# A hybrid decoder layer on one core: two token tiles first in the load queue, compressed-branch sums for four offsets at a time with a gate tile under them, and other places for the last rows of w_o

## The chip, the cores and the metric

The kernel runs on one core of one Trainium2 chip. The metric is the device time of one execution in microseconds (us); lower is better. TensorE multiplies matrices into PSUM, VectorE (DVE), ScalarE (ACT) and GpSimd (POOL) work elementwise, and SyncE (SP) issues most of the loads and stores; each engine takes its instructions in one fixed order.

## The reference

One decoder layer over 1024 tokens of width 1024, all in float32. What matters here:

```python
u = rmsnorm(h, norm_mix_pre[i])
(qa, ka, va, za, ba, aa, qb, kcm, vcm, ksl, vsl, kwi, vwi, gnsa, gmix) = \
    jnp.split(u @ w_in[i], offs, axis=-1)
ya = gdn_mixer(qa, ka, va, za, ba, aa, ...)      # chunked gated delta rule
yb = nsa_mixer(qb, kcm, vcm, ksl, vsl, kwi, vwi, gnsa, ...)   # sparse attention
g_a, g_b = jnp.split(jax.nn.sigmoid(gmix), 2, axis=-1)
mixed = (g_a * (ya @ w_a2d[i]) + g_b * (yb @ w_b2d[i])) @ w_o[i]
h = h + rmsnorm(mixed, norm_mix_post[i])
...                                               # gated MLP, per-layer embedding
def compress_blocks(x, pos, w1, w2):              # for k_cmp and for v_cmp
    ...                                           # blocks of 32 tokens, every 16 tokens: 63 of them
    blocks = blocks + pos[:, None, :]
    flat = jnp.moveaxis(blocks, 3, 2).reshape(B, nc, G, CMP_LEN * d)   # 2048 wide
    return jax.nn.gelu(flat @ w1) @ w2
```

## The kernel before

Every float32 product is split in three. A weight or activation is loaded as float32 ("raw"), ScalarE rounds it to a high part ("hi", whi, w_oh), and VectorE or GpSimd subtracts to get a low part ("lo", wlo, w_ol; all of these are line 313). `mm3` (lines 345 to 347) then issues hi·hi, hi·lo and lo·hi. `stream` does this for one strip of a weight matrix, in the tags "raw", "hi" and "lo" of the pool `wp`, two places each; `weights` does it for the weights `ws` of 288 columns, `resident` for whole rows of a matrix that stay.

The order of the instructions on each engine is laid out when the program is built, by a scheduler that goes by program order, by a simulated timeline and by when a tile's place is free. `tc.issue_after(at)` puts the TensorE instructions of a block behind the instruction `at`; this is how work of one stage is laid under another. A generator such as `project` yields after each half of a product, so a caller can take one step at a time.

*Start.* For each of eight tiles of 128 tokens: x is loaded (two places), normed (`norm_to_T`), turned on TensorE (pT_u) into uh and ul, and multiplied by `ws` (psm, 24 matmuls). All x and `ws` loads stand on SP's queue, as do the strips of w_in (raw) for the projections (pj) that follow. The strips `ws` are loaded in tile 0, after x of token tile 0: four tiles of two row blocks, three pieces each.

*Compressed branch* (`compress`, lines 1106 to 1150). For k and then v, 16 steps m of 128 rows of w1 each: X = one strided slice of cmr plus one column of the position weights (line 1119, VectorE, tile cx), then two matmuls with X (line 1121, tile ph). w1 comes two steps at a time. The generator yields after every four steps, eight times in all; at each yield two steps of the filler generator `first()` follow: q tiles 0 and 1 and one k tile, 12 steps. Then come the gelu (hT), the small product pc, and attention.

*Attention.* 64 items (two groups, eight query tiles, two head pairs, two branches), each with a front (scores ps, softmax Pt) and a back (transposes pt, products po). Under them runs `under()`: two q tiles, the remaining gate tiles of the generator `filler`, the product with w_a2d, and six turns of yb. The share that is due after each item is reckoned by `n_work` (286 units, five for each step) against the cost of the items.

*Merge and output projection.* The products with w_b2d (pab) come in four pairs, each pair with one `stream` of 512 KB; gates gt are loaded from DRAM through four and six buffers, and the merged rows go to mxh and mxl. `open_wo` makes rows 0 to 3 of w_o (k blocks of 128 rows) before that loop, and `ffn` makes rows 4 to 7 after it, in a pool woB, through the two places of "raw". Then `product(t, half)` multiplies token tiles 0 to 2 with rows 0 to 3 (half 0), then with rows 4 to 7 (half 1), 24 matmuls each, into pwo.

Of the kernel before, what the change touches and what calls it, by code (L numbers as in the profile page):

```python
# [7 lines left out]
F32 = mybir.dt.float32  # L8
F32R = mybir.dt.float32r
AF = mybir.ActivationFunctionType  # L10
ALU = mybir.AluOpType
# [4 lines left out]
P = 128  # L16
SEQ = 1024
NT = SEQ // P
DM = 1024
KD = DM // P  # L20
# [12 lines left out]
NWO = 4  # L33


def rows_to_all(ap, n, offset=0):
    return bass.AP(tensor=ap.tensor, offset=ap.offset + offset, ap=[[0, P], [1, n]])
# [257 lines left out]
class Body:  # L295
# [138 lines left out]
    def mixers(self, es_out):  # L434
        nc, tc, io = self.nc, self.tc, self.io
        win = self.dram2d("w_in", DM, DIN)
# [16 lines left out]
        uh = up.tile([P, KD, SEQ], F32R, name="uh")  # L453
        ul = up.tile([P, KD, SEQ], F32R, name="ul")
# [5 lines left out]
        with ExitStack() as e2:  # L460
            sp = self.pool(e2, "ws")
            xw = self.pool(e2, "xw")
            wbc = sp.tile([P, DM], F32, name="wbc")
            for t in range(NT):
                x = xw.tile([P, DM], F32, name="xt", tag="xt", bufs=2)
                nc.sync.dma_start(x, io["x"][0, t * P:(t + 1) * P, :])
                if t == 0:
                    nc.scalar.dma_start(wbc, rows_to_all(io["norm_mix_pre"], DM))
                self.norm_to_T(x, wbc, uh, ul, t, xw, self.psg, f"u{t}")
                if t == 0:  # L470
                    ws = [self.weights(sp, win, k * P, 2, 0, 288, f"ws{k}", 1, pieces=[
                        (0, OFF_VSL, 128), (128, OFF_VWI, 152), (280, OFF_BA, 8)], lo_eng=nc.vector)
                        for k in range(0, KD, 2)]
                    self.load_rows_T([(io["conv_qkv"], 48), (io["cmp_pos_k"], 16), (io["cmp_pos_v"], 16),
                                      (io["gdn_norm"], 1)], self.psg, sp, self.cvw)

                ps = self.psg.tile([P, 512], F32, name="psm", tag="g")
                s = slice(t * P, t * P + P)
                for k in range(KD):
                    self.mm3(ps[:, 0:288], uh[:, k, s], ul[:, k, s], *[w[:, k % 2] for w in ws[k // 2]], k == 0, k == KD - 1)  # L480
                nc.vector.tensor_copy(self.vv[:, t], ps[:, 0:256])
                nc.vector.tensor_copy(self.sg[:, t], ps[:, 256:288])

        def run_all(gen):
            for _ in gen:
                pass
# [49 lines left out]
        def project(off, evac):  # L536

            wh, wl = self.stream(win, 0, KD, off, P)
            for th in range(2):
                s = slice(th * 512, th * 512 + 512)  # L540
                ps = psF[0].tile([P, 512], F32, name="pj", tag="f")
                for k in range(KD):
                    self.mm3(ps, wh[:, k], wl[:, k], uh[:, k, s], ul[:, k, s], k == 0, k == KD - 1)
                    if k == 3:
                        yield
                evac(ps, s)
                yield
# [9 lines left out]
        def gates():  # L557
            for n in range(4, 20):
                yield from gate_tile(n)

        filler = gates()
# [3 lines left out]
        NG = 8  # L565
        self.gdn_prep(0)
        nfill = 0
        for c in range(NC):
            at = self.gdn_scan(c, gates_d, ya_d)
            if c + 1 < NC:  # L570
                at = at, self.gdn_prep(c + 1)
            else:
                at = at, at
# [32 lines left out]
        def q_tile(i):  # L606
            def evac(ps, s):
                for hf in range(2):
                    r = slice(hf * 64, hf * 64 + 64)
                    nc.scalar.activation(self.qb[r, i, s], ps[r], AF.Copy, scale=float(2.0 ** (2 * i + hf + 1) / 8.0))  # L610
            return project(OFF_QB + i * P, evac)
# [3 lines left out]
        def k_tile(n):  # L615
            return project((OFF_KSL, OFF_KWI)[n], lambda ps, s: nc.scalar.activation(self.kk[n][:, s], ps, AF.Copy))

        def first():
            for i in range(2):
                yield from q_tile(i)  # L620
            yield from k_tile(1)

        run_all(k_tile(0))
        fq = first()
        for at in self.compress():
            with tc.issue_after(at):
# [68 lines left out]
            wbs.extend(self.stream(wbd, 0, 4, f * P, 2 * P) for f in (0, 2))  # L695

        todo = under()
        n_work = 5 * (8 + 4 * (16 - NG) + 16) + 6
        cost = lambda i, br: (i + 2 if br == 1 else min(i + 1, 5)) + 1
        total = 4 * sum(cost(i, br) for i in range(NT) for br in (1, 2))  # L700
        items = [(g, i, pr, br) for g in range(2) for i in range(NT) for pr in range(2) for br in (1, 2)]
# [2 lines left out]
        for it in items:  # L704
            g, i, pr, br = it
# [4 lines left out]
            at = self.nsa_front(*it)  # L710
# [39 lines left out]
        for f0 in range(0, KD, 2):  # L750
            wb = wbs.pop(0)
            for th, f in ((0, f0), (0, f0 + 1), (1, f0), (1, f0 + 1)):
                s = slice(th * 512, th * 512 + 512)
# [150 lines left out]
    def gdn_inverse32(self):  # L904
# [6 lines left out]
        self.blk = blk = gp.tile([P, 4, H, P], F32, name="blk")  # L911
        Ls, X = [blk[:, 2 * i:2 * i + 2].rearrange("p a h k -> p (a h k)").rearrange("p (i j) -> p i j", j=32)
                 for i in range(2)]
        tmp = gp.tile([P, 256], F32, name="tmp", tag="T1")
        for hf in range(2):
# [20 lines left out]
            pp = slice(hf * m_, hf * m_ + m_)  # L936
            X_ = X[pp]
            nc.vector.memset(X_, 0.0)
# [166 lines left out]
    def compress(self):  # L1105

        nc, io = self.nc, self.io
        npl = self.pool(self.ces, "cmp")
        for n, s in enumerate("kv"):
            w1 = io[f"cmp_w1_{s}"]  # L1110
            ph = [self.pss.tile([P, 2, NCMP], F32, name="ph", tag="s") for _ in range(2)]
            for m0 in range(0, 16, 2):
                wt = npl.tile([P, 2, 256], F32, name="w1t", tag="w1t", bufs=2)
                nc.sync.dma_start(wt, bass.AP(tensor=w1.tensor, offset=w1.offset + m0 * P * 256,
                                              ap=[[256, P], [P * 256, 2], [1, 256]]))
                for m in (m0, m0 + 1):
                    X = npl.tile([P, 2, 63], F32, name="cx", tag="cx", bufs=2)
                    o = 48 + n * 16 + m
                    nc.vector.tensor_scalar(X, self.cmr[n][:, :, m:m + 497:8], self.cvw[:, o:o + 1], None, ALU.add)
                    for ht in range(2):  # L1120
                        at = nc.tensor.matmul(ph[ht][:, :, 0:63], wt[:, m - m0, ht * P:ht * P + P], X, start=m == 0,
                                              stop=m == 15).ins
                if m0 % 4 == 2:
                    yield at
            hT = npl.tile([P, 2, 2, NCMP], F32, name="hT", tag="hT", bufs=1)
            nc.vector.memset(hT, 0.0)
            for ht in range(2):
                nc.scalar.activation(hT[:, ht, :, 0:63], ph[ht][:, :, 0:63], AF.Gelu_apprx_tanh)
            w2 = npl.tile([P, 2, 2, 64], F32, name="w2t", tag="w2t", bufs=1)
            a = io[f"cmp_w2_{s}"]  # L1130
            for d in range(2):
                nc.sync.dma_start(w2[:, :, d], bass.AP(tensor=a.tensor, offset=a.offset,
                                                       ap=[[64, P], [P * 64, 2], [1, 64]]))
            pc = self.pst.tile([P, 2, NCMP], F32, name="pc", tag="t")
            if s == "k":
                for ht in range(2):
                    nc.tensor.matmul(pc, w2[:, ht], hT[:, ht], start=ht == 0, stop=ht == 1)
                nc.scalar.activation(self.khc, pc, AF.Copy)
                nc.vector.tensor_sub(self.klc, pc, self.khc.bitcast(F32))
            else:  # L1140
                h2 = npl.tile([P, 4, 2, NCMP], F32, name="h2", tag="h2", bufs=1)
                nc.vector.tensor_copy(h2, hT.rearrange("p a b n -> p (a b) n").unsqueeze(2).to_broadcast(
                    [P, 4, 2, NCMP]))
                for g in range(2):
                    for ht in range(2):
                        nc.tensor.matmul(pc[:, g], h2[:, ht * 2 + g].rearrange("p a n -> p (a n)"), w2[:, ht, 0],
                                         start=ht == 0, stop=ht == 1)
                nc.scalar.activation(self.vsc[:, :, 0:64], pc, AF.Copy)
                nc.vector.tensor_sub(self.vsc[:, :, 64:128], pc, self.vsc[:, :, 0:64].bitcast(F32))
        self.ces.close()  # L1150
# [195 lines left out]
    def ffn(self, es_out):  # L1346
        nc, io = self.nc, self.io
# [6 lines left out]
        wq = self.wq = self.pool(hes, "wq", side="right")  # L1354
        cv = wq.tile([P, 4, 2 * NF], F32, name="cv")
        wp = self.pool(self.wes, "woB")
        self.wo += self.resident(wp, "w_o", range(NWO, KD))
        wpost = wp.tile([P, DM], F32, name="wpost")
        nc.scalar.dma_start(wpost, rows_to_all(io["norm_mix_post"], DM))
        wpre = wp.tile([P, DM], F32, name="wpre")  # L1360
# [36 lines left out]
        for t in range(NT):  # L1397
            s = slice(t * P, t * P + P)
            x = wp.tile([P, DM], F32, name="x2", tag="x2", bufs=2)
# [250 lines left out]
```

## Time and profile before

| | |
|---|---|
| three runs, median | 1972.2 us (1970.51 to 1972.72) |
| the profiled execution: its time, its span | 1981.25 us, 1979.5 us |
| instructions | 25890 |
| mean granted clock of TensorE | 0.97 |

The span runs from the first to the last instruction of the profiled execution. Durations are read from it. PE is TensorE's matmul row, PEld its weight loads, which overlap it. A timeline row gives the start, the duration, the engine, the source line, the operation, what it writes and reads, its shape and its count; brackets give the idle time of the engine before it and what ended that. A matmul of 512 columns lasts about 0.39 us, but the next one starts 0.23 us after it.

### The profile page before, as it was taken

What the parts mean: (1) busy time and instruction counts of PE and PEld (TensorE: products, weight loads), DVE (VectorE), ACT (ScalarE), POOL (GpSimd) and SP (SyncE); (2) the same over time, 40 slices, a digit from 0 to 9 for tenths busy, and PEclk for the clock granted to TensorE, in tenths of its full rate; (3) what the DMA queues carried; (4) which work ended last, traced back from release to release, by engine and by line L of the source; (5) the groups of instructions that cost most, each with busy time, mean ns of one, the idle gap of its engine ahead of it and who ended that gap; (6) DMA issues with size and microseconds to landing.
All of it is one profiled execution on the core that took longest, in us unless ns stands there. A gap on an engine that the chain in (4) does not pass through costs nothing. (4 is left out here: it accounts for less than half of the span.)

```text
span 1979.5 us, 25890 instructions
## 1 busy us (share of the span) xinstructions
PE 1856.0 (94%) x9247; PEld 1537.6 (78%) x9247; DVE 1235.3 (62%) x2365; ACT 921.9 (47%) x1818; POOL 702.0 (35%) x537
## 2 busy tenths in 40 slices
PE   7999989999989999999999969999999999999998
PEld 6788778888878878778777857787877877777786
DVE  4437943341367667686684488776867774868643
ACT  4344223333267667676663234444444444346432
POOL 2132212223122212231153045666766665545200
PEclk9998989999989999999999979999999999999999
DMA  5124333323310110110063212323332348236201
GB/s 163 33 72 123 81 98 85 92 76 88 98 33 17 43 38 28 42 61 22 22 223 133 82 64 65 117 91 101 104 104 91 101 142 284 80 111 227 98 35 43
DMA packets 182847, 178.68 MB, mean 90 GB/s; under 512 B 27773, under 2 KB 133566, under 8 KB 182718
## 3 DMA queue, kind: packets, MB, share of 16 engines
q1 hardware_dynamic: 180496, 170.33, 27.5%
q10 hardware_dynamic: 2222, 6.69, 0.9%
q8 instruction: 73, 1.20, 0.2%
q14 instruction: 56, 0.46, 0.1%
HBM read 132.65 MB, written 44.34 MB: 89 GB/s over the span
## 5 line engine op out<-in xcount | busy, mean ns | idle before, releaser
L345 PE MATMUL pj<-uh,whi 128*128 128x512 f32 x640 | 263.5, 412 | 7.5 <-DVE y L515 5.8
L347 PE MATMUL pj<-uh,wlo 128*128 128x512 f32 x640 | 258.9, 404 | 0.0
L346 PE MATMUL pj<-ul,whi 128*128 128x512 f32 x640 | 258.6, 404 | 0.0
L313 POOL TENSOR_TENSOR wlo<-raw,whi 128x1024 fp32r<-128x1024 f32 x48 | 116.9, 2437 | 324.6 <-ACT whi L324 263.8
L345 PEld LDWEIGHTS pj<-uh,whi 128*128 128x128 f32 x640 | 123.7, 193 | 34.6 <-issue 4.4
L313 POOL TENSOR_TENSOR whl<-s,whl 128x512 fp32r<-128x512 f32 x88 | 126.4, 1444 | 59.0 <-ACT whl L1331 59.0
L347 PEld LDWEIGHTS pj<-uh,wlo 128*128 128x128 f32 x640 | 123.3, 193 | 29.0
L346 PEld LDWEIGHTS pj<-ul,whi 128*128 128x128 f32 x640 | 123.8, 193 | 26.1
L313 POOL TENSOR_TENSOR wdhl<-wd,wdhl 128x512 fp32r<-128x512 f32 x66 | 99.0, 1510 | 80.4 <-ACT wdhl L1331 78.9
L313 POOL TENSOR_TENSOR whl<-raw,whl 128x512 fp32r<-128x512 f32 x66 | 105.3, 1597 | 50.9 <-ACT whl L1331 50.3
L313 DVE TENSOR_TENSOR whl<-araw,whl 128x512 fp32r<-128x512 f32 x77 | 86.7, 1133 | 55.3 <-ACT whl L1331 55.2
L345 PE MATMUL q<-mxh,whl 128*128 128x512 f32 x264 | 104.8, 400 | 3.4 <-ACT u L106 2.2
L1243 DVE TENSOR_TENSOR Tl<-pt,Th 128x512 fp32r<-128x512 f32 (+1 forms) x152 | 92.6, 617 | 23.6 <-ACT Th L1242 19.8
L1213 ACT ACTIVATE Pt<-Pt,nm 128x640 f32<-128x640 f32 (+7 forms) x128 | 93.0, 728 | 30.2 <-DVE nm L1211 29.7
L346 PE MATMUL q<-mxl,whl 128*128 128x512 f32 x264 | 104.9, 397 | 0.0
L347 PE MATMUL q<-mxh,whl 128*128 128x512 f32 x264 | 104.1, 397 | 0.2 <-POOL whl L313 0.2
L1242 ACT ACTIVATE Th<-pt 128x512 fp32r<-128x512 f32 (+1 forms) x152 | 79.2, 538 | 51.7 <-PE po L1246 35.6
L324 ACT ACTIVATE whi<-raw 128x1024 fp32r<-128x1024 f32 x48 | 50.5, 1053 | 80.3 <-PE pj L346 54.4
L1239 PE MATMUL pt<-ident,Pt 128*128 128x128 f32 x528 | 82.9, 277 | 2.9 <-DVE Tl L1243 1.3
L126 DVE SCALAR_TENSOR_TENSOR yg<-c,cv,yg 128x1 f32<-128x1 f32 (+2 forms) x88 | 81.3, 928 | 0.9 <-ACT yg L123 0.9
L1331 ACT ACTIVATE whl<-s 128x512 fp32r<-128x512 f32 x88 | 54.7, 624 | 56.9 <-PE n L347 44.1
L1205 PE MATMUL ps<-kst,qs 128*128 128x512 f32 (+3 forms) x192 | 70.4, 369 | 6.7 <-DVE mx L1208 4.9
(533 smaller groups left out, 5138.7 us busy)
## 6 DMA issues: line engine op xcount, KB each, us to landing
raw<-in_w_up SPq DMA_DIRECT2D x44, 512.0 KB
raw<-in_w_in SPq DMA_DIRECT2D x40, 512.0 KB
araw<-acts SPq DMA_DIRECT2D x35, 512.0 KB
acts<-sd SPq DMA_DIRECT2D x44, 256.0 KB
gates_d<-yz SPq DMA_DIRECT2D x40, 256.0 KB
acts<-yv SPq DMA_DIRECT2D x33, 256.0 KB
gt<-gates_d SPq DMA_DIRECT2D x32, 256.0 KB
wd<-in_w_down SPq DMA_DIRECT2D x7, 1024.0 KB
```

Source lines behind the costliest of these rows:

```text
L126: self.body.nc.vector.scalar_tensor_tensor(y, src, w, y, ALU.mult, ALU.add)
L313: return eng.tensor_sub(lo, src, hi.bitcast(F32)).ins
L324: nc.scalar.activation(hi, raw, AF.Copy)
L345: nc.tensor.matmul(ps, lh, rh, start=start, stop=False, skip_group_check=more)
L346: nc.tensor.matmul(ps, lh, rl, start=False, stop=False, skip_group_check=more)
L347: nc.tensor.matmul(ps, ll, rh, start=False, stop=stop, skip_group_check=more)
L1205: nc.tensor.matmul(ps[:, 0:n], qs[:, hh], kh, start=True, stop=False)
L1213: nc.scalar.activation(Pt[:, hh, 0:nk], Pt[:, hh, 0:nk], AF.Exp, scale=2.0 ** -(h0 + hh + 1), bias=nm[:, br, hh:hh + 1], accum_out=rs[:, b ...
L1239: nc.tensor.transpose(pt[:, b, hh], Pt[:, hh, (b0 + b) * P:(b0 + b + 1) * P], self.ident)
L1242: nc.scalar.activation(Th[:, 0:m], pt[:, 0:m], AF.Copy)
L1243: nc.vector.tensor_sub(Tl[:, 0:m], pt[:, 0:m], Th[:, 0:m].bitcast(F32))
L1331: self.nc.scalar.activation(hi, src, AF.Copy)
```

## The change

Four edits. x of token tiles 0 and 1 is put on SP's queue ahead of the strips `ws`, and those come as two tiles of four row blocks (three pieces each) in place of four tiles of two. In `compress`, w1 comes four steps at a time, X is made for four steps by two additions of two tensors (one for each of the two groups g), and the clearing of hT is cut to its one padded column. After q and k tiles, `first()` goes on with four steps of `filler`, that is with one gate tile, and `n_work` counts one gate tile less (266 units). Rows 6 and 7 of w_o are loaded into a place of the tags "hi" and "lo" of `wp`, where the merge's w_b2d parts lie, and rows 4 and 5 into "raw" as before.

```diff
--- before.py
+++ after.py
@@ -461,23 +461,32 @@
             sp = self.pool(e2, "ws")
             xw = self.pool(e2, "xw")
             wbc = sp.tile([P, DM], F32, name="wbc")
+            xs = {}
+
+            def load_x(t):
+                xs[t] = xw.tile([P, DM], F32, name="xt", tag="xt", bufs=2)
+                nc.sync.dma_start(xs[t], io["x"][0, t * P:(t + 1) * P, :])
+
+            load_x(0)
+            load_x(1)
             for t in range(NT):
-                x = xw.tile([P, DM], F32, name="xt", tag="xt", bufs=2)
-                nc.sync.dma_start(x, io["x"][0, t * P:(t + 1) * P, :])
+                if t > 1:
+                    load_x(t)
+                x = xs.pop(t)
                 if t == 0:
                     nc.scalar.dma_start(wbc, rows_to_all(io["norm_mix_pre"], DM))
                 self.norm_to_T(x, wbc, uh, ul, t, xw, self.psg, f"u{t}")
                 if t == 0:
-                    ws = [self.weights(sp, win, k * P, 2, 0, 288, f"ws{k}", 1, pieces=[
+                    ws = [self.weights(sp, win, k * P, 4, 0, 288, f"ws{k}", 1, pieces=[
                         (0, OFF_VSL, 128), (128, OFF_VWI, 152), (280, OFF_BA, 8)], lo_eng=nc.vector)
-                        for k in range(0, KD, 2)]
+                        for k in range(0, KD, 4)]
                     self.load_rows_T([(io["conv_qkv"], 48), (io["cmp_pos_k"], 16), (io["cmp_pos_v"], 16),
                                       (io["gdn_norm"], 1)], self.psg, sp, self.cvw)
 
                 ps = self.psg.tile([P, 512], F32, name="psm", tag="g")
                 s = slice(t * P, t * P + P)
                 for k in range(KD):
-                    self.mm3(ps[:, 0:288], uh[:, k, s], ul[:, k, s], *[w[:, k % 2] for w in ws[k // 2]], k == 0, k == KD - 1)
+                    self.mm3(ps[:, 0:288], uh[:, k, s], ul[:, k, s], *[w[:, k % 4] for w in ws[k // 4]], k == 0, k == KD - 1)
                 nc.vector.tensor_copy(self.vv[:, t], ps[:, 0:256])
                 nc.vector.tensor_copy(self.sg[:, t], ps[:, 256:288])
 
@@ -619,6 +628,8 @@
             for i in range(2):
                 yield from q_tile(i)
             yield from k_tile(1)
+            for _ in range(4):
+                yield next(filler)
 
         run_all(k_tile(0))
         fq = first()
@@ -695,7 +706,7 @@
             wbs.extend(self.stream(wbd, 0, 4, f * P, 2 * P) for f in (0, 2))
 
         todo = under()
-        n_work = 5 * (8 + 4 * (16 - NG) + 16) + 6
+        n_work = 5 * (8 + 4 * (15 - NG) + 16) + 6
         cost = lambda i, br: (i + 2 if br == 1 else min(i + 1, 5)) + 1
         total = 4 * sum(cost(i, br) for i in range(NT) for br in (1, 2))
         items = [(g, i, pr, br) for g in range(2) for i in range(NT) for pr in range(2) for br in (1, 2)]
@@ -1109,21 +1120,23 @@
         for n, s in enumerate("kv"):
             w1 = io[f"cmp_w1_{s}"]
             ph = [self.pss.tile([P, 2, NCMP], F32, name="ph", tag="s") for _ in range(2)]
-            for m0 in range(0, 16, 2):
-                wt = npl.tile([P, 2, 256], F32, name="w1t", tag="w1t", bufs=2)
+            for m0 in range(0, 16, 4):
+                wt = npl.tile([P, 4, 256], F32, name="w1t", tag="w1t", bufs=2)
                 nc.sync.dma_start(wt, bass.AP(tensor=w1.tensor, offset=w1.offset + m0 * P * 256,
-                                              ap=[[256, P], [P * 256, 2], [1, 256]]))
-                for m in (m0, m0 + 1):
-                    X = npl.tile([P, 2, 63], F32, name="cx", tag="cx", bufs=2)
-                    o = 48 + n * 16 + m
-                    nc.vector.tensor_scalar(X, self.cmr[n][:, :, m:m + 497:8], self.cvw[:, o:o + 1], None, ALU.add)
+                                              ap=[[256, P], [P * 256, 4], [1, 256]]))
+
+                X = npl.tile([P, 4, 2, 63], F32, name="cx", tag="cx", bufs=2)
+                v = self.cmr[n].rearrange("p g (n m) -> p m g n", m=8)[:, m0 % 8:m0 % 8 + 4, :, m0 // 8:m0 // 8 + 63]
+                o = 48 + n * 16 + m0
+                for g in range(2):
+                    nc.vector.tensor_tensor(X[:, :, g], v[:, :, g], self.bc(self.cvw[:, o:o + 4], 63), ALU.add)
+                for m in range(m0, m0 + 4):
                     for ht in range(2):
-                        at = nc.tensor.matmul(ph[ht][:, :, 0:63], wt[:, m - m0, ht * P:ht * P + P], X, start=m == 0,
-                                              stop=m == 15).ins
-                if m0 % 4 == 2:
-                    yield at
+                        at = nc.tensor.matmul(ph[ht][:, :, 0:63], wt[:, m - m0, ht * P:ht * P + P], X[:, m - m0],
+                                              start=m == 0, stop=m == 15).ins
+                yield at
             hT = npl.tile([P, 2, 2, NCMP], F32, name="hT", tag="hT", bufs=1)
-            nc.vector.memset(hT, 0.0)
+            nc.vector.memset(hT[:, :, :, 63:64], 0.0)
             for ht in range(2):
                 nc.scalar.activation(hT[:, ht, :, 0:63], ph[ht][:, :, 0:63], AF.Gelu_apprx_tanh)
             w2 = npl.tile([P, 2, 2, 64], F32, name="w2t", tag="w2t", bufs=1)
@@ -1354,7 +1367,8 @@
         wq = self.wq = self.pool(hes, "wq", side="right")
         cv = wq.tile([P, 4, 2 * NF], F32, name="cv")
         wp = self.pool(self.wes, "woB")
-        self.wo += self.resident(wp, "w_o", range(NWO, KD))
+        for ks, tag in (((4, 5), "raw"), ((6,), "hi"), ((7,), "lo")):
+            self.wo += self.resident(wp, "w_o", ks, place=(self.wp, tag))
         wpost = wp.tile([P, DM], F32, name="wpost")
         nc.scalar.dma_start(wpost, rows_to_all(io["norm_mix_post"], DM))
         wpre = wp.tile([P, DM], F32, name="wpre")
```

## Rows read from the trace of the kernel before

**Rows 1.** The page, part 1: busy time, share of the span, instructions.
```profile
PE 1856.0 (94%) x9247; PEld 1537.6 (78%) x9247; DVE 1235.3 (62%) x2365; ACT 921.9 (47%) x1818; POOL 702.0 (35%) x537
```

**Rows 2.** Timeline of SyncE's queue, start: start us, us, what.
```profile
1.25 9.60 SPq L334 DMA_DIRECT2D raw_ws<-in_w_in  x12
10.89 0.94 SPq L466 DMA_DIRECT2D xt<-in_x  x2
```

**Rows 3.** Timeline of all engines, start; in brackets idle before and releaser.
```profile
13.86 0.68 ACT L338 ACTIVATE hi_ws<-raw_ws 128x576 fp32r<-128x576 f32 x1 [1.18 <-DMA raw_ws<-in_w_in]
...
14.58 0.76 DVE L313 TENSOR_TENSOR lo_ws<-raw_ws,hi_ws 128x576 fp32r<-128x576 f32 x1 [0.98 <-ACT hi_ws L338]
...
19.21 1.06 PE L374 MATMUL pT_u<-ident,xs_u 128*128 128x128 f32 x8 [2.90 <-DVE ra_u L353]
...
26.00 0.29 PE L346 MATMUL psm<-lo_ws,uh 128*128 128x288 f32 x1
...
26.14 0.29 PE L347 MATMUL psm<-hi_ws,ul 128*128 128x288 f32 x1
```

**Rows 4.** DMA view, first 40 us: GB/s in slices of one us.
```profile
GB/s 0 16 254 287 416 328 81 136 157 133 203 209 142 256 373 336 344 328 258 111 135 369 160 291 137 215 245 199 315 273 217 173 352 70 12 0 0 0 123 377
```

**Rows 5.** Timeline of TensorE, compressed branch.
```profile
512.89 2.19 PE L1121 MATMUL ph<-cx,w1t 128*128 128x126 f32 x16
...
520.52 2.19 PE L1121 MATMUL ph<-cx,w1t 128*128 128x126 f32 x16
522.46 0.48 PE L345 MATMUL pj<-uh,whi 128*128 128x512 f32 x1
...
531.96 0.82 PE L1121 MATMUL ph<-cx,w1t 128*128 128x126 f32 x4 [1.63 <-DVE cx L1119]
...
535.94 0.39 PE L347 MATMUL pj<-uh,wlo 128*128 128x512 f32 x1
...
547.30 2.19 PE L1121 MATMUL ph<-cx,w1t 128*128 128x126 f32 x16
551.38 1.13 PE L1121 MATMUL ph<-cx,w1t 128*128 128x126 f32 x8 [1.89 <-DVE cx L1119]
554.09 2.08 PE L1121 MATMUL ph<-cx,w1t 128*128 128x126 f32 x8 [1.58 <-DVE cx L1119]
...
560.29 0.44 PE L1205 MATMUL ps<-kst,qs 128*128 128x128 f32 x1 [1.32 <-issue]
...
567.07 0.22 PE L1205 MATMUL ps<-kst,qs 128*128 128x128 f32 x1
```

**Rows 6.** Line 1119, the sums X: ns min/median/max, first and last start.
```profile
L1119 DVE TENSOR_SCALAR cx<-cm,cvw x32: 320/334/2225, 477.9 to 554.0; 128x126 f32<-128x126 f32 x32
```

**Rows 7.** Timeline of all engines, the first of the late sums.
```profile
529.24 2.91 DVE L1119 TENSOR_SCALAR cx<-cm,cvw 128x126 f32<-128x126 f32 x3
529.29 2.48 POOL L313 TENSOR_TENSOR wlo<-raw,whi 128x1024 fp32r<-128x1024 f32 x1 [12.73 <-ACT whi L324]
```

**Rows 8.** Attention in 22 stretches of 20 us: two of them, and the sum.
```profile
580.00:600.00 20.00, 18.44 (x110) 15.60 (x109) 16.01 (x61) 15.70 (x48) 6.18 (x9) 1.00 0.11 27
...
780.00:800.00 20.00, 17.95 (x112) 15.36 (x110) 17.23 (x74) 16.51 (x55) 8.36 (x9) 0.97 0.11 34
...
sum 440.00, PE 419.52 PEld 355.25 DVE 307.57 ACT 302.25 POOL 98.67; mean PE 19.07 PEld 16.15 DVE 13.98 ACT 13.74 POOL 4.48
```

**Rows 9.** Timeline of TensorE, start of the output projection.
```profile
1046.84 0.39 PE L345 MATMUL pwo<-w_oh,mxh 128*128 128x512 f32 x1
...
1069.49 1.65 PE L345 MATMUL pwo<-w_oh,mxh 128*128 128x512 f32 x3 [3.42 <-ACT w_oh L1310]
...
1075.18 0.40 PE L347 MATMUL pwo<-w_oh,mxl 128*128 128x512 f32 x1
```

**Rows 10.** Timeline of ScalarE, the same stretch.
```profile
1054.88 1.06 ACT L1310 ACTIVATE w_oh<-raw 128x1024 fp32r<-128x1024 f32 x1 [0.84 <-DVE mxl L313]
...
1068.38 1.06 ACT L1310 ACTIVATE w_oh<-raw 128x1024 fp32r<-128x1024 f32 x1 [11.50 <-DMA raw<-in_w_o]
```

## The prediction

> **What bounds the kernel now.** I read the page's busy times first: TensorE is busy for 94% of the span and no other engine for more than 62% [rows 1]. So the time is TensorE's work plus its pauses, 124 us of them (1979.5 less 1856.0), and a change that leaves the matmuls alone can only earn pauses, or stretches in which matmuls are spaced as at the lower of the clock's two levels. The reader should look at three places, because the change has one part in each. At the start [rows 2 to 4] the weights wait for the DMA queue and the second token tile waits behind them. In the compressed branch [rows 5 to 7] the filler runs out two steps of the generator before the branch does, and TensorE then waits for VectorE. At the start of the output projection [rows 9, 10] TensorE waits for the last rows of w_o. Between the last two lies attention, 440 us in which TensorE is busy for 419.5 [rows 8]; it matters because the change takes filler out of it.
>
> **Part 1, the start.** Nothing is computed differently. SP issues 12 loads of ws over 9.6 us and only then the second token's x [rows 2]. The last quarter of ws is rounded at 13.86 and its low part is ready at 15.34 (14.58 plus 0.76) [rows 3]; the first tile's matmuls can then end, and TensorE waits 2.90 us until 19.21 for the second token's norm. That token's last matmul starts at 26.14 [rows 3]. After the change x of token 1 is ahead of ws, so its norm and transposes lie under the wait for ws; in exchange ws comes later by one load of 512 KB and in halves instead of quarters. In the slices of one us that follow the first loads 254 to 416 GB/s moved [rows 4]; 0.52 MB at 350 GB/s is 1.5 us. So the second half lands 1.5 us later, at about 15.4. Rounding it takes ScalarE about 1.2 us, estimated from 0.68 us for a tile of half the size, and VectorE about 1.4, from 0.76: 18.0. Eleven of token 0's 24 matmuls are left then (the second half's twelve, less the first, which needs no low part), 1.5 us at the spacing of 0.13 to 0.14 us that its neighbour at 26.00 has to 26.14. Token 1 follows at once: 24 matmuls, 3.2 us, and token 2's 8 transposes, 1.0 us (as token 1's at 19.21), which had also been done by 26.14. That gives 23.7, a gain of 2.4 us. I take off 1.4 because matmuls that begin after a longer wait will run at the lower clock longer: gain 1.0 us. Bounds: +4 if x1 costs ws nothing and the clock is up in time; -2 if the halves come a further 3 us late. Third and later x loads still wait for a place of two, and the w_in loads stand behind them on SP as before; TensorE has projections to do from then on, so I price that at nothing, and at 1 us if that cover were gone (it is in the bounds).
>
> By the Trainium skill, "DMA: Bandwidth & Descriptors", section "Queues, rings and completion order", a DMA engine takes the descriptors of one queue's ring in order; by that ws waits for all of x1 and the sum for this part stays at 1.0. If the two shared the engines instead, so that ws lost nothing, it would be 2.5 by the same working. No row here separates the two.
>
> **Part 2, the compressed branch.** Eight groups of 16 matmuls run, four for k and four for v, and after each two filler steps. One group with its filler takes 7.63 us (512.89 to 520.52), of which 1.94 the group and 5.69 the two steps [rows 5]. There are 12 steps of filler, so groups 7 and 8 had none. The change adds four, one gate tile, so that all eight are covered.
>
> What is removed. (a) At 531.96 TensorE has waited 1.63 us for X. From there to 535.94 four sums (0.48 us) and eight filler matmuls start; the eight take 3.5 us where 5.69 for 24 would make it 1.9. Together 3.2. The cause is visible on VectorE: X takes 0.33 us at the median but 2.2 at the most [rows 6], and just here three of them take 2.91 us, beside a rounding by GpSimd of 2.48 [rows 7]. X had two buffers of one offset each, so it could be made only one offset ahead. (b) From 547.30 to 567.07 are 19.77 us [rows 5]. The work in them at the full clock: 32 sums at 1.94 per 16, 3.9; 16 matmuls of pc and ps, about as wide as the sums, 1.9; 12 filler matmuls, 2.85. That is 8.65, so 11.1 are lost, in waits of 1.89, 1.58 and 1.32 us and a few under 1 us, and in half-clock matmuls. With the gate tile under groups 7 and 8 and X made four offsets at a time and two groups ahead (7.6 us ahead, against a worst X of 2.5), all of it closes except the wait of 1.32 before the first scores, where pc, the rounding of q and the scores follow each other and no filler is queued. I let that wait cost 1.0 more in clock. So 3.2 + 11.1 - 1.3 - 1.0 = 12.0 us.
>
> What is added. The X sums are 2 instructions on VectorE for 4 offsets instead of 4; at 252 elements each I estimate 0.4 us, from 0.33 us for 126, so VectorE does less, and it is off the path. The w1 loads are 8 of 512 KB in place of 16 of 256 KB, with as many bytes; two groups are ahead, 15 us for a load, so nothing. The smaller memset is off the path too. The gate tile brings one w_in load, one rounding by ScalarE and GpSimd (2.5 us) and two stores on SP, all of which were in attention; on SP they go ahead of the last w1 loads, whose cover is the same 7.6 us.
>
> What is given back. The four steps, 11.4 us, leave attention. Its 64 items share 56 steps of filler now and 52 afterwards, so 12 instead of 8 items go without. Over 440 us TensorE pauses 20.5 us there [rows 8]. Four more items, at 0.3 us (the mean pause for each item) to 1.3 (the wait before the first scores [rows 5]), are 1 to 5 us; I take 3. So attention shrinks by about 8.4 of the 11.4, and part 2 earns 9.0. Bounds: 13.0 with no clock loss and nothing reopened; 0.6 if attention does not shrink at all.
>
> **Part 3, w_o.** Rows 4 to 7 are loaded through two places of "raw". Their rounding can begin at 1054.88, when VectorE has done the last mxl, because only then the tiles for them are free [rows 10]. So raw is held until then, rows 6 and 7 are loaded after it, and row 6 is rounded at 1068.38 after 11.50 us of idle time on ScalarE that a DMA ended [rows 10]. TensorE starts the first half at 1046.84; 84 matmuls (72 of the first half, 12 of rows 4 and 5) last until 1066.07, 0.23 us each. It waits 3.42 us until 1069.49, and 13 matmuls until 1075.18 take 5.69 us instead of 2.97 [rows 9]: 3.42 + 2.72 = 6.1 lost. After the change rows 6 and 7 are loaded into places that the merge's third weight pair gives back; 48 merge matmuls before 1046.84, at 0.23 us, put that at about 1035.6, so the loads are there by 1054.88. Four roundings of 1.06 us end by 1059.1, and the low parts (1.4 us on VectorE, estimated from 0.76 for 576 columns [rows 3], and 2.5 on GpSimd as in [rows 7], two each) by about 1062 to 1064. Row 6 is wanted at 1066.1, row 7 at 1067.5. Gain 6.0; bounds 6.1 and 0 (the loads go out only after 1054.88 all the same). SP's wait for those two places stands ahead of at most the last gate loads; those have four and six buffers.
>
> **Sum.** 1.0 + 9.0 + 6.0 = 16.0 us. The profiled execution took 1981.25 us (span 1979.5), so it would take 1965. The median of the runs shown is 1972.2, 9.05 lower; the same difference gives **1956 us**.
>
> **The rivals.** *A, the forecast*, 1949 to 1962; chance 0.50. *B, attention does not shrink*: VectorE and ScalarE are the real limit there, filler was free, and its 11.4 us come back as pauses. For it: VectorE and ScalarE are each busy around 70% [rows 8]. Against: TensorE is at 95%. 1.0 + 0.6 + 6.0 = 7.6: 1964.6 us; chance 0.17. *C, X stays late*: VectorE makes X only just before use, and GpSimd still holds it up, so that (a) and the wait of 1.89 with its clock remain, about 6 us: 1962 us; chance 0.12. The Trainium skill, "SBUF — State Buffer", section "Who interferes with whom", speaks for it: a VectorE instruction with two SBUF inputs is blocked by a GpSimd instruction that reads SBUF for the whole of it, and the new X has two SBUF inputs. The trace agrees that X was held up as long as GpSimd ran [rows 6, 7]. *D, part 3 does not happen*, because rows 6 and 7 are still issued only after 1054.88: 1.0 + 9.0 = 10.0, 1962 us; chance 0.10. *E, slower*: in attention the clock falls. Two stretches of 20 us show it: 18.44 busy still had a granted clock of 1.00, 17.95 had 0.97 [rows 8]. With less filler more stretches look like the second. One hundredth over 440 us costs 4.4 us, so from a fall of the mean by 0.036 on the 16.0 are gone, and a fall by 0.055 makes 1980. Against: even the second stretch, the emptiest before 980, has 0.97, and 11.4 us less in 440 moves the busy share by 2.6% at most. Chance 0.07. *F*, the instruction order changes elsewhere and eats it, within 4 us of before; 0.04.
>
> **How the numbers follow.** The time is that of A, 1956. A's own range is 1949 to 1962: the upper bounds of the parts (4 + 13.0 + 6.1) would give 1949. B, C and D lie at 1962 to 1965, so 1949 to 1967 leaves out about 0.11 for E and F and some tails of the others. A measurement of this kernel tells about 0.2%, 4 us, from no change. Faster needs less than 1968: A to D, less a part of B's and D's tails, 0.83. Slower by 0.2%: E and a little of F, 0.07. Same: 0.10.
>
> **What will show it.** Right: TensorE's rows have no wait for X, and after group 8 comes a gate tile's pj; attention's pauses rise by less than 5 us from 20.5; no TensorE wait for w_oh, and row 6's load is issued before 1050; the second token's transposes come before the first token's last psm. Wrong: attention is as long as before (B); X rows of 2 us next to TensorE waits (C); an SP load of w_o behind w_up (D); a mean granted clock that falls by over 0.03 in attention (E). What I cannot see is the order that instructions get on each engine; if it moves work in stages that the diff does not touch, the forecast fails there.

## The result and the profile after

The changed kernel takes 1958.95 us at the median of nine runs (1954.95 to 1967.18), the kernel before 1973.14 in nine runs taken in turn with them. The ratio is 0.9921 [0.9906, 0.9935], which is 15.6 us less (14.2 by the two medians). The forecast was 1956 us, 16.2 less. The profiled execution took 1955.27 us, its span 1953.5. The page's busy times, as in [rows 1]: TensorE 20.8 us less.

```profile
PE 1835.2 (94%) x9247; PEld 1522.0 (78%) x9247; DVE 1226.0 (63%) x2347; ACT 919.8 (47%) x1816; POOL 708.2 (36%) x537
```

One execution of one kernel differs from the next by several us (spans of 1962.5 to 1975.9 us among 35 runs of the kernel before), so a stage's length is compared below over several profiles. Windows of the changed kernel by stage: compressed branch (first ph to first ps), attention (to the last po), merge (to the first pwo), output projection (to the last pwo). After the time come the busy times of the engines, then the granted clock, DMA share and GB/s.

```profile
479.10:553.70 74.60, 71.77 (x381) 60.69 (x379) 19.34 (x22) 24.65 (x40) 14.58 (x7) 1.00 0.30 87
553.70:978.00 424.30, 403.01 (x2445) 341.56 (x2446) 298.66 (x1060) 295.86 (x764) 95.37 (x115) 0.99 0.10 32
978.00:1031.30 53.30, 47.49 (x198) 37.40 (x197) 45.70 (x50) 33.42 (x55) 30.61 (x18) 0.97 0.71 237
1031.30:1121.90 90.60, 90.60 (x418) 75.35 (x417) 41.78 (x68) 27.99 (x60) 17.80 (x19) 1.00 0.31 106
```

The same stages of the kernel before, repeated (the experiment with no edit):

```profile
478.10:550.40 72.30, 65.05 (x334) 54.13 (x332) 23.19 (x40) 21.60 (x35) 12.32 (x5) 0.95 0.33 90
550.40:984.20 433.80, 415.48 (x2493) 352.34 (x2494) 304.12 (x1060) 299.27 (x769) 97.92 (x116) 0.98 0.11 33
984.20:1037.30 53.10, 48.94 (x197) 38.53 (x196) 45.63 (x50) 33.32 (x55) 30.70 (x18) 0.94 0.64 218
1037.30:1131.70 94.40, 92.56 (x418) 76.26 (x417) 40.56 (x68) 28.24 (x60) 16.89 (x19) 0.98 0.32 113
```

The branch has become longer, since it holds 11.4 us more filler, and attention shorter; the two together take 498.9 us for 506.1. The reader should watch the clock column beside the idle time: the branch loses 4.4 us of idle time and its clock goes from 0.95 to 1.00.

*Start.* Rows of SyncE, ScalarE and TensorE, which answer to [rows 2, 3]:

```profile
0.80 0.87 SPq L468 DMA_DIRECT2D xt<-in_x  x2
1.72 7.44 SPq L334 DMA_DIRECT2D raw_ws<-in_w_in  x6
...
12.58 1.17 ACT L338 ACTIVATE hi_ws<-raw_ws 128x1152 fp32r<-128x1152 f32 x1
12.67 1.91 PE L374 MATMUL pT_u<-ident,xs_u 128*128 128x128 f32 x8
...
21.37 1.03 PE L374 MATMUL pT_u<-ident,xs_u 128*128 128x128 f32 x8
...
24.64 0.63 PE L374 MATMUL pT_u<-ident,xs_u 128*128 128x128 f32 x4 [1.45 <-DVE xs_u L365]
```

The wait of 2.90 us for the second token tile's norm is gone: that tile is turned at 12.67, under the wait for ws, and the third tile at 21.37. The next long wait is for VectorE's next norm (1.45 us). The second half of ws is rounded at 12.58, before the last quarter of [rows 3] at 13.86; the row has no idle time, so ScalarE did not wait for this load.

*Branch.* TensorE's timeline for [rows 5]; then ScalarE, VectorE and GpSimd ahead of the first scores:

```profile
505.08 1.95 PE L1135 MATMUL ph<-cx,w1t 128*128 128x126 f32 x16
...
512.48 1.94 PE L1135 MATMUL ph<-cx,w1t 128*128 128x126 f32 x16
...
549.89 1.06 ACT L324 ACTIVATE whi<-raw 128x1024 fp32r<-128x1024 f32 x1 [5.14 <-PE pj L346]
...
551.02 2.34 POOL L313 TENSOR_TENSOR wlo<-raw,whi 128x1024 fp32r<-128x1024 f32 x1 [12.40 <-ACT whi L324]
551.33 0.27 ACT L1161 ACTIVATE vsc<-pc 128x128 fp32r<-128x128 f32 x1
551.48 1.72 ACT L1191 ACTIVATE qs<-qb 64x256 fp32r<-64x256 f32 x4
...
552.00 2.52 DVE L313 TENSOR_TENSOR qs<-qb,qs 64x256 fp32r<-64x256 f32 x2
...
553.75 0.30 PE L1218 MATMUL ps<-kst,qs 128*128 128x128 f32 x1 [2.87 <-issue]
...
554.57 0.33 PE L1218 MATMUL ps<-kst,qs 128*128 128x128 f32 x1 [0.41 <-DVE qs L313]
```

A group of 16 matmuls takes 1.95 us and no group waits. But the wait before the first scores, 1.32 us in [rows 5], has grown to 2.87 + 0.41. VectorE's two low parts of qs took 0.87 us in the kernel before and take 2.52 here. The row of before:

```profile
559.77 0.87 DVE L313 TENSOR_TENSOR qs<-qb,qs 64x256 fp32r<-64x256 f32 x2 [0.17 <-ACT qs L1178]
```

The sums X, beside [rows 6]:

```profile
L1132 DVE TENSOR_TENSOR cx<-cm,cvw x16: 626/660/2694, 469.8 to 530.2; 128x252 f32<-128x252 f32 x16
```

They still take up to 2.69 us, and nobody waits.

*Output projection*, SyncE and ScalarE, for [rows 10]:

```profile
1026.05 0.86 SPq L1320 DMA_DIRECT2D raw<-in_w_o  x2
...
1039.13 1.06 ACT L1323 ACTIVATE w_oh<-raw 128x1024 fp32r<-128x1024 f32 x1 [0.84 <-DVE mxl L313]
...
1041.05 1.99 ACT L1323 ACTIVATE w_oh<-raw 128x1024 fp32r<-128x1024 f32 x2
```

SyncE in the kernel before:

```profile
1057.53 5.96 SPq L1307 DMA_DIRECT2D raw<-in_w_o  x2
```

The last two loads go out at 1026.05, 5 us before the stage begins (before at 1057.53, some 11 us behind its begin), the four roundings follow one another, and TensorE has no pause in the stage (90.60 of 90.60 us).

### The profile page after: what moved, and what is told of

Same layout as the page of the kernel before. It is cut to its first block, busy times and chain, and to the rows that moved or that the text cites. A ratio compares the mean times of both kernels' runs of the same rounds, so it can differ in the third digit from the quotient of the medians.

```text
span 1953.5 us, 25809 instructions
## 1 busy us (share of the span) xinstructions
PE 1835.2 (94%) x9247; PEld 1522.0 (78%) x9247; DVE 1226.0 (63%) x2347; ACT 919.8 (47%) x1816; POOL 708.2 (36%) x537
## 5 line engine op out<-in xcount | busy, mean ns | idle before, releaser
L313 POOL TENSOR_TENSOR whl<-s,whl 128x512 fp32r<-128x512 f32 x88 | 131.6, 1505 | 57.2 <-ACT whl L1344 57.2
L1294 POOL TENSOR_TENSOR tm<-tm 128x128 f32<-128x128 f32 x32 | 14.7, 460 | 196.2 <-DVE tm L1292 160.8
```

Source lines behind the costliest of these rows:

```text
L313: return eng.tensor_sub(lo, src, hi.bitcast(F32)).ins
L1294: nc.gpsimd.tensor_add(tm[:, 0], tm[:, 0], tm[:, 1])
```

## The experiments

**Each part alone.** The kernel before once more; the start edit alone; the sums and the gate tile alone; the places of w_o alone.

> The kernel before, unchanged, taken once more. Spread theory (the two profiled executions, 1979.5 and 1953.5, lie 26 us apart while the medians lie 14 us apart, because executions of one kernel differ by some us in stages that nothing touches): a span some 4 to 10 us below 1979.5, ratio 1.000, and the first sums of the compressed branch begin 2 to 6 us ahead of 486.4. Start theory (the start edit is worth 7 us, as the first sums' 486.4 against 479.1 suggest): they begin within 1 us of 486.4 again.

> Only the start edit: two x tiles first in the queue and ws in two halves. Spread theory: 1 to 3 us faster than before (ratio 0.998 to 1.0), and what the first 25 us of the trace gain is what stays. Start theory: about 7 us faster, ratio 0.9965.

> Only the sums for four offsets, the gate tile under them and the filler count. Forecast: 9.0 us faster, ratio 0.9954, attention shorter by 8 to 9 us. Rival B (attention does not shrink): 0.6 us, ratio 0.9997. Rival C (sums stay late): about 3 us, ratio 0.9985.

> Only the places of w_o rows 6 and 7. Forecast: 6.0 us faster, ratio 0.997, and no wait of TensorE for w_oh. Rival D (the loads still go out late): ratio 1.000.

The kernel before took 1971.7 us beside these four. No edit: 0.9999 [0.9986, 1.0013]. Start: 1.0000 [0.9988, 1.0013]. Sums and gate tile: 0.9965 [0.9951, 0.9979], 6.9 us less. w_o: 0.9988 [0.9975, 1.0002], 2.4 us less. The unchanged kernel's profile has a span of 1963.7 for 1979.5 us and its first sums at 478.1 for 486.4: more than was expected of the spread, and not the start edit's doing.

The sum of the parts, 9.3 us, is short of 15.6, by only a little more than the intervals allow. The profile of the start edit shows one reason: its merge took 56.2 us where the kernel before took 53.0 and 53.1. TensorE waits there for a rounding of the next weights, 4.18 us, where it waited 2.36 to 2.44 for a product of the gates before, and its clock in the merge is 0.91 for 0.94. VectorE's products of the gates stand in another order than before. The lines, TensorE in the merge, of the start edit, then of the changed kernel:

```profile
1015.94 0.80 PE L345 MATMUL pab<-ybh,whi 128*128 128x512 f32 x1 [4.18 <-ACT whi L324]
```
```profile
1008.61 0.50 PE L345 MATMUL pab<-ybh,whi 128*128 128x512 f32 x1 [4.00 <-DVE gt L769]
```

So an edit at the start re-orders work 900 us later. The changed kernel has VectorE's order of before, waits 4.00 us at this place as well, and its merge takes 53.3 at a clock of 0.97: the wait alone is not the 3 us. With w_o alone its stage takes 90.7 us at a clock of 1.00, as in the changed kernel.

**The two halves of part 2.** Sums without the gate tile: X and w1 as in the change, `first()` and `n_work` as before. From its diff against the kernel before:

```diff
-            for m0 in range(0, 16, 2):
...
+            for m0 in range(0, 16, 4):
...
+                for g in range(2):
+                    nc.vector.tensor_tensor(X[:, :, g], v[:, :, g], self.bc(self.cvw[:, o:o + 4], 63), ALU.add)
```

> X and w1 for four offsets at a time, without the gate tile. If late X is what costs (part 2, a, and the X waits of 1.89 and 1.58 us in groups 7 and 8), TensorE has no wait of over 0.3 us for cx, and the kernel is 3.2 to 7 us faster, the rest of the 11.1 us staying because nothing lies under groups 7 and 8 and the gelu. If X stays late beside GpSimd (rival C), waits for cx of 1 us and more remain and the time is within 2 us of before.

0.9946 [0.9933, 0.9959], 10.6 us less: more than with the gate tile (the intervals overlap), and more than the 3.2 to 7 that were expected. In the branch it is 7.6 us; the merge, which the edit does not touch, took 51.1 us for 53.0. Windows (branch, attention) and TensorE's timeline:

```profile
485.20:549.90 64.70, 60.84 (x334) 51.77 (x332) 18.16 (x22) 21.44 (x35) 11.95 (x5) 0.99 0.33 92
549.90:982.90 433.00, 414.67 (x2493) 351.78 (x2494) 304.61 (x1060) 299.15 (x769) 97.71 (x116) 0.99 0.10 33
```
```profile
541.20 3.73 PE L1124 MATMUL ph<-cx,w1t 128*128 128x126 f32 x32
...
547.53 1.10 PE L1148 MATMUL pc<-w2t,h 128*128 128x64 f32 x8 [2.61 <-DVE h L1144]
549.89 0.45 PE L1207 MATMUL ps<-kst,qs 128*128 128x128 f32 x1 [1.25 <-issue]
```

Groups 7 and 8, with nothing under them, take 3.73 us together: X is ready. What is left is 2.61 us behind the gelu and 1.25 before the scores. The gate tile with the sums as before (`first()` and `n_work` alone):

> The gate tile under groups 7 and 8 and n_work less by 20, with X and w1 as before. If missing filler is what costs, the branch loses its pauses behind group 6 (about 7.9 us of 11.1 gross) and attention gives 3 us back: about 5 us faster, with the X waits of rows 5 (1.63 us) left. If filler was free in attention (rival B), attention stays at 433.8 us, the branch becomes some 4 us longer, and the time is the same or up to 4 us longer than before.

0.9988 [0.9975, 1.0], 2.4 us less. Windows (branch, attention) and the wait that stays:

```profile
481.20:561.20 80.00, 75.52 (x381) 62.48 (x380) 24.47 (x40) 24.68 (x40) 14.98 (x7) 0.98 0.32 88
561.20:988.30 427.10, 405.35 (x2445) 343.89 (x2446) 298.20 (x1060) 296.12 (x764) 95.33 (x115) 0.98 0.10 32
```
```profile
526.77 0.71 PE L1123 MATMUL ph<-cx,w1t 128*128 128x126 f32 x4 [1.63 <-DVE cx L1121]
```

The two stages together take 507.1 us: nothing won. The expected 5 us did not come.

**The changed kernel again, and the wait before the scores.**

> The changed kernel unchanged, once more. If the three parts add up as they were measured alone (0.0, -7.2 and -1.5 us), the ratio is 0.995 to 0.996. If the first result of 0.9921 stands, the parts together save about 6 us more than alone, and the granted clock of attention will again be about 0.99 against 0.98.

0.9923 [0.9906, 0.9939]: the first result stands. Branch 74.6, attention 427.5 us at a clock of 0.98; so attention of this one kernel differs by 3 us and 0.01 of clock between two executions. The first query tile's qs made earlier (comments added here):

```diff
+            if n == 4:                         # behind group 5
+                self.nsa_q(0, 0)
...
     def nsa_q(self, g, i):
-        nc, npl = self.nc, self.np_            # a pool that is made behind the branch
+        nc, npl = self.nc, self.nsar           # a pool that is open in the branch
```

> The changed kernel with the first query tile's rounding (qs of group 0, tile 0) made under group 5 of the compressed branch, not behind pc. If qs is what the 2.87 us before the first scores wait for, this wait and the 0.41 behind it fall to under 0.5 us, the clock in the 20 us that follow rises from 0.91 to about 1.00, and the kernel is 3 to 5 us faster than the changed one in the same call. Rival: the first scores wait for pc and its copies instead, or the pause moves behind the first softmax, which has no filler either; then it is within 1 us of the changed kernel.

0.9909 [0.9892, 0.9926]; by the medians 2.3 us under the repeat of the changed kernel, measured beside it, where 3 to 5 were expected (the intervals overlap). The branch takes 71.6 us, all of them busy:

```profile
479.00:550.60 71.60, 71.60 (x382) 60.62 (x380) 19.20 (x21) 23.16 (x37) 13.61 (x7) 1.00 0.30 87
```

The 3.28 us are gone from the branch, and no further wait opened in it. So qs was what the scores waited for. The clock in the 20 us behind the first scores did not rise to 1.00 as expected: it is 0.91, as in the first profile of the changed kernel (0.83 in its repeat).

**Without the gate tile, and the filler spread.** The changed kernel less the gate tile; then also, with qs early:

```diff
-                next(fq, None)
-                next(fq, None)
+                for _ in range((1, 1, 1, 2, 1, 2, 2, 2)[n]):
+                    next(fq, None)
+            if n == 5:
+                self.nsa_q(0, 0)
```

> The changed kernel without the gate tile in the branch (first() and n_work as before); start, sums and w_o as changed. If the gate tile earns nothing once X comes early (the branch grows by 9.9 us with it, attention shrinks by 6.3 on average), this is 2 to 5 us faster than the changed kernel: ratio to before 0.990 to 0.991, branch 64.7 us, attention 433. If the forecast's working holds (the tile closes pauses that X alone leaves, and 8.4 of 11.4 us come back), it is 3 to 6 us slower than the changed kernel: ratio 0.9945 to 0.996.

> The changed kernel without the gate tile; the 12 filler steps stand behind the eight groups as 1, 1, 1, 2, 1, 2, 2, 2, so that two of them lie under each of the two chains gelu to pc, and the first qs is made under group 6. If the pauses of 2.61 and 1.25 us that the sums alone left (behind gelu, and before the first scores) are all that is left in the branch, it takes 60 to 61 us with TensorE busy throughout, attention 433, and the kernel is about 4 us faster than without the gate tile alone, 1950 to 1953 us by the time of before in these calls. Rival: with only one step between groups X or w1 comes late (waits for cx or the load of 0.5 us and more), and the branch stays at 64 to 66 us.

Without the tile 1955.96 us, 0.9912 [0.9892, 0.9933], 2 to 3 us under the changed kernel; its branch takes 65.5 us, attention 433.8. That is on the side of no gain from the tile, though the intervals overlap. Its windows (branch, attention):

```profile
479.40:544.90 65.50, 61.68 (x333) 52.55 (x331) 18.14 (x22) 21.40 (x35) 11.96 (x5) 0.97 0.33 91
544.90:978.70 433.80, 415.33 (x2493) 352.32 (x2494) 304.33 (x1060) 299.43 (x769) 97.91 (x116) 0.98 0.10 33
```

Spread: 1952.08 us, **0.9887 [0.9866, 0.9908]**, the fastest kernel here, 21 us under before. Windows and timeline of it:

```profile
478.20:538.60 60.40, 60.40 (x333) 51.61 (x332) 14.14 (x19) 18.97 (x32) 11.23 (x6) 1.00 0.33 90
538.60:972.30 433.70, 414.64 (x2495) 351.32 (x2495) 307.30 (x1062) 301.02 (x772) 98.92 (x115) 0.99 0.11 34
```
```profile
537.80 1.00 PE L1159 MATMUL pc<-w2t,h 128*128 128x64 f32 x8
538.61 0.31 PE L1218 MATMUL ps<-kst,qs 128*128 128x128 f32 x1
...
542.77 0.34 PE L1218 MATMUL ps<-kst,qs 128*128 128x128 f32 x2
```

The same twelve steps as before cover the branch whole: one step between two groups is enough for X, and two lie under each gelu. 60.4 us is what was expected.

**The start.** Only x of two tiles first, ws in quarters; and the spread kernel with quarters.

> Only x of token tiles 0 and 1 first in the queue; ws in quarters as before. In the four profiles with the whole start edit the last psm ends at 62.9 and the first gate scores of the linear attention come at 80.8 to 81.3; without it at 63.4 to 66.0 and at 79.6 to 87.3. If the order of x does this, psm ends at 62.9 or earlier and the second stage begins by 81. If the halves of ws do it (six issues in 7.44 us for twelve in 9.60), psm ends at 64 or later. In time both are within 3 us of before.

> As the kernel with the spread filler, but ws in quarters again: x of two tiles first, twelve pieces of ws behind it. If the 5.0 us that the order of x saved alone belong to the start (against 0.0 with halves), this is 2 to 5 us faster than with halves: ratio to before 0.986 to 0.988, with a second stage that begins before 81. If halves are the better (12.58 against 14.61 for the rounding of the last piece) the second stage begins 2 to 5 us later, at 83 to 86, and the ratio is 0.989 to 0.991. If the 5.0 lay in a later stage (the linear attention took 170.3 against 172.5 to 177), the ratio stays within 0.001 of 0.9887.

0.9975 [0.9959, 0.9991], 5.0 us where at most 3 were expected, and 0.9918 [0.9897, 0.994]. SyncE and ScalarE of the first of the two:

```profile
1.71 10.71 SPq L334 DMA_DIRECT2D raw_ws<-in_w_in  x12
...
14.61 0.68 ACT L338 ACTIVATE hi_ws<-raw_ws 128x576 fp32r<-128x576 f32 x1 [1.13 <-DMA raw_ws<-in_w_in]
```

With quarters behind two x tiles the last quarter is rounded at 14.61 and 14.76, the second stage (first pss) begins at 86.3 and 84.8 us; with halves it begins at 80.8 to 81.3 in six profiles, with the old start at 79.6 to 87.3 (mean 84.0) in six. So the order of x alone gains nothing here, and with the halves it is about 3 us on average; the halves with the old order were not run.

Against that, the linear attention (first pz to last pu) took 170.3 and 170.7 us in these two kernels and 172.5 to 177.2 in all others, which is about where the 5.0 us of the first come from. The traces show how: TensorE's instructions stand there in another order in these two (the same in both), and its waits for T (tile pu) come to 3.5 and 3.7 us, in all others to 6.0 to 8.3. Why this edit leads to that order, no run separates. What was expected of halves at the second stage's begin held. The spread kernel with quarters is 3 us slower by the medians, but the intervals overlap, and its merge, with VectorE in the order of the start edit alone, took 55.4 us for 51.3.

## Why the prediction held in sum and not in its terms

**Part 1, forecast 1.0 us.** The second tile's transposes did move ahead of the first tile's products, as forecast. The third tile's were done at 22.4 us where the sum said 23.7, because the halves did not land 1.5 us later: the second was rounded at 12.58 (12.55 to 12.65 in six profiles), against 12.89 to 13.97 for the last quarter in six profiles with the old start. The step that failed is this delay. It priced the 0.52 MB of x and gave nothing for fewer pieces. The bytes do cost: with quarters behind two x tiles the last one came at 14.61 and 14.76, 1.2 us later than the mean of the old start, 13.5. The Trainium skill, "DMA: Bandwidth & Descriptors", section "Queues, rings and completion order", by which each DMA engine takes the descriptors of one ring in order, agrees in sign. The halves outweighed it: six pieces were issued by 9.16 us, twelve by 10.85 [rows 2], or by 12.42 behind two x; and ScalarE waited for a load with quarters, but not with halves. The second stage began about 3 us earlier on average (the kernel before alone had 85.8 and 79.6). As a time of the whole kernel the start alone gained 0.0 us [-2.6, 2.4], while its profile shows 3 us more in the merge. Its worth lies between 0 and 3.

**Part 2, forecast 9.0 us.** The change measured 6.9 alone. Here the mechanism was wrong in one step: (b) charged 11.1 us to groups 7 and 8 being without filler and to X together, and let the gate tile cover them. The runs part the two. X four at a time, two buffers of four, closes 7.6 of the 11.9 us that lie between the old branch (72.3) and the spread one (60.4), with no filler added and attention unchanged. Left for the tile were 2.61 us behind the gelu; it covered those, and lengthened the wait before the scores from 1.25 to 3.28. The forecast said that no filler is queued there and kept 1.32. It overlooked the gate tile's own queue: ScalarE takes the next weights' rounding (whi) ahead of qs and, in its fixed order, waits 5.14 us for whi's place, and beside GpSimd's wlo of 2.34 us VectorE's two qs take 2.52 (0.87 in the kernel before). How the 3.28 divide between the two was not measured. The Trainium skill, "SBUF — State Buffer", section "Who interferes with whom", has that case: two inputs from SBUF on VectorE beside a GpSimd instruction that reads SBUF. The trace agrees here, and for X, whose longest takes 2.69 us; there it was hidden.

The stretch of (b) also reached 6.8 us into attention (560.29 to 567.07), where by its own prices the work is 3.8: 3.0 of the 11.1 lie there, out of the gate tile's reach. The spread kernel runs this piece in 4.2 us (538.61 to 542.77) at a clock of 1.00, but has 0.91 in the 20 us from 558.6, and its attention is no shorter (433.7).

*Given back.* Attention takes 433.0 to 434.0 us in eight profiles with the tile left in it (430.9 in one more) and 424.3, 424.3, 427.1, 427.5 and 429.7 in five without: 7 us less on average for 8.4 forecast. Its idle time is 18.3 to 19.2 us with and 20.4 to 22.8 without, about the 3 us that were assumed. But the branch grows by 9.5 for the tile (64.7 and 65.5 against 74.6 and 74.7), and TensorE's wait for the gates in the merge is 3.4 to 4.0 us in the five, 1.9 to 2.4 in the seven others whose VectorE has the same order there. Moved, the tile costs 2 to 3 us once X is early.

**Part 3, forecast 6.0 us.** The mechanism was right: no wait for w_oh, clock 1.00. The size was that of the one execution, 97.0 to 90.6. The mean of seven profiles with the old places is 95.1, which makes 4.5; the time of this part alone says 2.4 [-0.4, 4.9].

**The rivals.** B fell: attention shrank. C: X is still held up, but two groups ahead it costs nothing; with the old sums its wait of 1.63 stayed under the gate tile as well. D: the loads go out at 1026.05. E: the clock in attention did not fall (0.98 to 0.99 for 0.98). F happened, in both directions, though in neither of these stages of the changed kernel: 3 us more in the merge with the start edit alone, 3 less in the linear attention with only the order of x.

So 1.0 + 9.0 + 6.0 came to about the right sum because a start that was taken too low made up for parts 2 and 3 taken too high; that is luck, not working. By stages over these profiles the parts give about 3 + 5 + 4.5 = 12.5 us; some 3 of the 15.6 [12.8, 18.5] are assigned to no stage. The signs that the forecast named for being right all came true. None of them asked what the branch would be without the gate tile, and that is where the step that failed lies.

## What to carry to other kernels

Before more filler is laid under a pause, make what the pause waits for earlier and deeper buffered, and see what is left: here four sums ahead took 7.6 us off the branch, and the filler moved under them gained nothing that the times show and cost 2 to 3 us by the stages. Filler brings its own roundings into the in-order queues of ScalarE and GpSimd; place the small instruction that opens the next stage ahead of them. And measure parts one by one with several profiles each, since an edit re-orders work far away: shifts of 3 us in stages that the diff does not touch were as large as the effects sought.

## What had not been expected of the hardware

The pauses of the branch cost more than their length: before, it had 7.25 us of idle time and lost 11.9 us against the spread kernel (72.3 to 60.4), the rest with the granted clock at 0.95 for 1.00. And for loads of the same bytes behind the same two x tiles, six issues took SyncE 7.44 us and twelve 10.71.
